# An MLP's up-projection by Strassen's scheme, and a down-projection of its own

## The chip, the cores and the metric

The kernel runs on one core of a Trainium2 chip. A core has five engines that run side by side, each with its own queue of instructions: TensorE (PE, matmuls, with the loads of its weights shown as PEld), VectorE (DVE), ScalarE (ACT), GpSimd (POOL) and SyncE (SP), which here issues the DMAs. They wait for one another by semaphores. The metric is the device time of one execution in microseconds (us); lower is better.

## The reference, cut to what matters

One encoder layer over 2048 tokens of 1024 features, in float32. The mixer and the cross-attention come first and are not touched. What is changed is the MLP behind them, with 4096 hidden features:

```python
def sq_relu_mlp(x, mlp_norm, w_up, w_down):
    h = rms_norm(x, mlp_norm) @ w_up          # 2048 x 1024 @ 1024 x 4096
    return jnp.square(jax.nn.relu(h)) @ w_down  # 2048 x 4096 @ 4096 x 1024

x = x + sq_relu_mlp(x, mlp_norm[l], w_up[l], w_down[l])
return rms_norm(x, final_norm)
```

## The kernel before, in words

Activations lie with features on the 128 partitions and tokens along the row. Float32 accuracy is made from reduced-precision operands: `split` (L108) turns a tensor into a high part (a cast on ACT, L110) and a low part, the remainder (a subtraction on DVE, L111), and `mm3` (L136) makes of each product three matmuls: high by high, high by low, low by high (L138 to L140). A matmul has 128 contracted rows and up to 512 columns.

The MLP (L952 on) takes the 2048 tokens in two halves (`hf`) of 1024, each of two blocks of 512. A half goes through 16 groups of two hidden feature tiles (128 features each). In a group, the up-projection makes one PSUM tile per hidden tile and block: 8 k-tiles by 3 matmuls. ACT takes the ReLU out of PSUM (L994), DVE multiplies it with the positive part (L996), and the result is split. Then the down-projection: for each block and each of the 8 output tiles `d`, 2 x 3 matmuls into PSUM, which DVE adds to a running sum in SBUF (L1029). These sums `acc` begin as the residual, which the cross-attention has stored in DRAM as `x2d`. Both weight matrices are loaded (512 KB a tile, L124) and split once per half, so twice in all.

The token operands are the normalised blocks. The 1/rms of a block is made by squares on ACT (`fold`, L177), their sums on GpSimd (L181), a small matmul (L154), a power on GpSimd (L146) and a broadcast by matmul (L162); the final norm does the same with squares of L1035 and sums of L1039. For the MLP's input, `prep_step` (L195) multiplies the block by it (L199) and splits it. For the first half this is done before the cross-attention's end: the loads, the products and the splits of block 0, and the first weights, stand ahead of `xa_last` (L717), the last piece of the cross-attention, which adds into the residual (L727) and stores it (L728). For the second half it is spread over the last groups of the first (L1004 to L1013, L1030 to L1032).

The order of the instructions is made by the framework's scheduler, which keeps one static queue for each engine; buffers come from pools of tiles with a fixed number of buffers, and a tile that is to be written waits for the last reader of the one that had the place before. PSUM has eight banks, four of the tag `ps` and four of `pg`. SP issues all loads and stores in one order, and an issue that waits holds up those behind it.

The lines that the prediction's steps touch:

```python
L110  mark["act"] = nc.scalar.copy(hi, src)
L111  nc.vector.tensor_tensor(out=lo, in0=src, in1=hi.bitcast(F32), op=ALU.subtract)
L994  nc.scalar.activation(r, ps, AF.Relu)
L996  nc.vector.scalar_tensor_tensor(out=u, in0=ps, scalar=0.0, in1=r, op0=ALU.max, op1=ALU.mult)
L1029 nc.vector.tensor_tensor(out=acc[d][:, cs], in0=ps, in1=acc[d][:, cs], op=ALU.add)
```

Of the kernel before, what the change touches and what calls it, by code (L numbers as in the profile page):

```python
# [30 lines left out]
def block_kernel(ctx, tc, x, mem, wm, wv, wlg, wlog, wout, wxk, wxv, wxqT, wxo, wup, wdn,  # L31
# [3 lines left out]
    big = ctx.enter_context(tc.tile_pool(name="big", bufs=1))  # L35
# [38 lines left out]
    # ---- constants  # L74
# [14 lines left out]
    nc.vector.tensor_copy(oneb, one)  # L89
    nhalf = cpool.tile([P, 16], F32, name="nhalf")  # L90
    nc.vector.memset(nhalf, -0.5)

    # ---- scratch in DRAM
# [8 lines left out]
    x2d = dram.tile([D, S], F32, name="x2d")  # L102

# [45 lines left out]
    def rstd_col(sq, PT):  # L149
        """sums of squares over the features, left on each partition -> 1 / rms, tokens on partitions"""  # L150
# [6 lines left out]
    def to_rows(rc, PT):  # L157
        """one value per token, tokens on partitions -> the same on all partitions"""
# [13 lines left out]
    def fold(tiles, SQ, eng):  # L172
        """squares of the tiles [P, 2, n], summed up"""
# [20 lines left out]
    def prep_step(res, gain, r, kp, xt):  # L194
        """two feature tiles of a block of 512 tokens, normalised: hi and lo [P, 2 kt, 512]"""  # L195
# [8 lines left out]
    # =========================== in-projection ===========================  # L204
# [4 lines left out]
    def mtiles(tiles, blks, ws=None):  # L209
        """tiles: (index, evac); the whole group for one block, then for the other one"""  # L210
# [44 lines left out]
    def vg(hf, blks, nxt, meanwhile=None):  # L255
        """columns of v and of silu(g), 256 at a time"""
# [8 lines left out]
    def lr_g(hf, blks):  # L265
        """low-rank gate inputs (rows f at 0..15, ones at 16, b at 32..47, b one token late) and g's first columns"""
# [32 lines left out]
    def conv(hf, blks, cs, ws=None, meanwhile=None):  # L299
        # y = B * dwconv3(C * u), channels on partitions  # L300
# [4 lines left out]
        def group(c, ws):  # L305
# [16 lines left out]
            def taps():  # L322
                # T[i] is the convolution at token (t0 + i) in the first half, (t0 - 2 + i) in the second
# [42 lines left out]
    # =========================== gated linear attention ===========================  # L366
    def gla_decay(h, res):
        """decayed k and q, rows 0..63 for the forward scan and 64..127 for the backward one; in stages"""
# [5 lines left out]
        # log_sigmoid(z) = min(z, 0) - ln(1 + exp(-|z|))  # L374
# [14 lines left out]
        def sums(hf):  # L389
# [5 lines left out]
            # sums run from token 0 and from token 64 of a chunk; both become distances to token 63  # L395
# [28 lines left out]
        # decay from one chunk's middle to the next one's  # L424
# [539 lines left out]
    for hf in range(2):  # L964
# [11 lines left out]
        for g in range(NG_):  # L976
            fs = range(G * g, G * g + G)
            if g > 0:
                ws = [load_w(wup[f]) for f in fs]
# [128 lines left out]
```

## Time and profile before

| what | value |
|---|---|
| three runs, us | 2854.97, 2857.62, 2862.69 (median 2857.62) |
| span of the profiled execution, first to last instruction, us | 2856.6 |
| mean granted TensorE clock | 0.983 of full speed |
| TensorE busy, us | 2756.2 (96%) |
| from the MLP's first matmul to the end, us | about 1435 |
| matmuls from 1422 us to the end | 6291 recorded |
| DVE, ACT and POOL busy from 1422 us to the end, us | 720, 317, 69 |
| DMA from 1422 us to the end | 20% busy, 62 GB/s |

The profiled execution is known by its span; the record of it holds no other time, and the span lies between the lowest and the highest of the three runs. A busy share alone does not say what sets the time: TensorE is nearly always busy, so what counts is how many matmuls there are, at what pitch they follow one another, and where TensorE stops.

### The profile page before, as it was taken

The numbers are of one execution on the slowest core, as the hardware profiler recorded it, in microseconds if no ns is written. First come the engines' busy times: TensorE is split into PE (matmuls) and PEld (weight loads), VectorE is DVE, ScalarE is ACT, GpSimd is POOL, SyncE is SP. The second block draws the span as 40 slices with busy tenths as digits, with TensorE's granted clock in tenths as the row PEclk, the third lists the DMA queues.
The fourth block names the chain that finished last, engine by engine and source line by source line (L and its number), as shares of the span: only waits on it lengthen the run. The fifth ranks groups of instructions, "written<-read, shape, count | busy, mean of one in ns | idle before, by whom it ended". The sixth has DMA issues, their size and how long they took to land.

```text
span 2856.6 us, 34634 instructions
## 1 busy us (share of the span) xinstructions
PE 2756.2 (96%) x14232; PEld 2352.7 (82%) x14232; DVE 1413.6 (49%) x2177; ACT 811.6 (28%) x1222; POOL 183.9 (6%) x149
## 2 busy tenths in 40 slices
PE   7999989988989999999999999999999999999997
PEld 6898878877777889999988888888878888888886
DVE  6413372556766544343554544444575454444444
ACT  5411162423445433221321121122232122112122
POOL 1000010302200000000200000002030000000003
PEclk9999999998999999999999999999999999999999
DMA  7412363234445441101621111122153111112111
GB/s 239 157 62 67 109 221 115 88 92 116 129 125 186 144 157 45 60 31 59 214 74 45 45 59 45 45 60 88 60 162 104 45 45 59 45 45 59 45 37 60
DMA packets 140383, 259.92 MB, mean 91 GB/s; under 512 B 12672, under 2 KB 69120, under 8 KB 140224
## 3 DMA queue, kind: packets, MB, share of 16 engines
q1 hardware_dynamic: 140224, 257.70, 28.8%
q8 instruction: 111, 1.82, 0.3%
q14 instruction: 48, 0.39, 0.0%
HBM read 203.13 MB, written 54.53 MB: 90 GB/s over the span
## 4 chain that ended last, share of the span: by engine, by line
PE 64%; issue 2%; DVE 2%; ACT 1%; POOL 1%; DMA 1%; SPq 0%; POOLq 0%; DVEq 0%; ACTq 0%
PE ps L138 11%; PE ps L139 11%; PE ps L140 11%; PE pg L140 10%; PE pg L138 10%; PE pg L139 10%; POOL gt L1039 0%; PE pg L698 0%; DMA raw<-zy 0%; DVE a L111 0%; POOL sm L146 0%; DVE raw L199 0%; PE ps L162 0%; DMA raw<-in_wout 0%; ACT L590 0%
## 5 line engine op out<-in xcount | busy, mean ns | idle before, releaser
L138 PE MATMUL ps<-a,a 128*128 128x512 f32 (+1 forms) x1864 | 706.3, 379 | 7.4 <-DVE t L242 6.7
L139 PE MATMUL ps<-a,a 128*128 128x512 f32 (+1 forms) x1864 | 705.6, 379 | 0.0
L140 PE MATMUL ps<-a,a 128*128 128x512 f32 (+1 forms) x1864 | 704.1, 378 | 0.0
L110 ACT CAST a<-raw 128x1024 fp32r<-128x1024 f32 (+1 forms) x216 | 219.5, 1033 | 702.1 <-PE pg L140 508.1
L138 PEld LDWEIGHTS ps<-a,a 128*128 128x128 f32 x1864 | 354.6, 190 | 74.1 <-DVE t L242 6.2
L111 DVE TENSOR_TENSOR a<-raw,a 128x1024 fp32r<-128x1024 f32 (+1 forms) x216 | 263.5, 1225 | 291.2 <-PE ps L139 205.6
L139 PEld LDWEIGHTS ps<-a,a 128*128 128x128 f32 x1864 | 355.0, 190 | 63.1 <-issue 0.2
L140 PEld LDWEIGHTS ps<-a,a 128*128 128x128 f32 x1864 | 354.7, 190 | 63.4 <-issue 0.4
L138 PE MATMUL pg<-gt,a 128*128 128x512 f32 (+1 forms) x880 | 302.8, 344 | 0.0
L140 PE MATMUL pg<-gt,a 128*128 128x512 f32 (+1 forms) x880 | 302.8, 344 | 0.0
L139 PE MATMUL pg<-gt,a 128*128 128x512 f32 (+1 forms) x880 | 302.7, 344 | 0.0
L1029 DVE TENSOR_TENSOR g<-pg,g 128x512 f32<-128x512 f32 (+1 forms) x260 | 177.3, 683 | 148.0 <-PE pg L140 147.9
L1029 DVE TENSOR_TENSOR st<-pg,st 128x512 f32<-128x512 f32 (+1 forms) x260 | 176.7, 681 | 118.5 <-PE pg L140 118.4
L138 PE MATMUL pg<-g,a 128*128 128x512 f32 (+1 forms) x552 | 213.8, 387 | 3.1 <-DVE st L1029 2.8
L139 PE MATMUL pg<-g,a 128*128 128x512 f32 (+1 forms) x552 | 213.4, 387 | 0.0
L140 PE MATMUL pg<-g,a 128*128 128x512 f32 (+1 forms) x552 | 213.3, 386 | 0.0
L994 ACT ACTIVATE t<-ps 128x512 f32<-128x512 f32 x128 | 76.6, 599 | 424.6 <-PE ps L140 424.6
L996 DVE SCALAR_TENSOR_TENSOR t<-ps,t 128x512 f32<-128x512 f32 x128 | 88.1, 688 | 204.2 <-ACT t L994 204.2
L138 PEld LDWEIGHTS pg<-gt,a 128*128 128x128 f32 x880 | 166.9, 190 | 20.2 <-DVE gt L111 0.3
L139 PEld LDWEIGHTS pg<-gt,a 128*128 128x128 f32 x880 | 167.0, 190 | 19.9
L140 PEld LDWEIGHTS pg<-gt,a 128*128 128x128 f32 x880 | 167.1, 190 | 19.6
L138 PEld LDWEIGHTS pg<-g,a 128*128 128x128 f32 x552 | 103.8, 188 | 24.6 <-DVE st L1029 3.1
(284 smaller groups left out, 3755.3 us busy)
## 6 DMA issues: line engine op xcount, KB each, us to landing
raw<-in_wup SPq DMA_DIRECT2D x64, 512.0 KB, 3.6
raw<-in_wdn SPq DMA_DIRECT2D x64, 512.0 KB, 3.9
raw<-in_wm SPq DMA_DIRECT2D x32, 512.0 KB, 4.1
raw<-x2d SPq DMA_DIRECT2D x48, 256.0 KB, 3.8
a<-in_x SPq DMA_DIRECT2D x32, 256.0 KB, 6.4
gt<-zv SPq DMA_DIRECT2D x32, 256.0 KB, 3.4
raw<-zy SPq DMA_DIRECT2D x32, 256.0 KB, 4.0
raw<-in_wv SPq DMA_DIRECT2D x12, 512.0 KB, 4.6
```

Of the source, the lines that this page charges most:

```text
L110: mark["act"] = nc.scalar.copy(hi, src)
L111: nc.vector.tensor_tensor(out=lo, in0=src, in1=hi.bitcast(F32), op=ALU.subtract)
L138: nc.tensor.matmul(ps, lh, rh, start=first, stop=False)
L139: nc.tensor.matmul(ps, lh, rl, start=False, stop=False)
L140: mark["pe"] = nc.tensor.matmul(ps, ll, rh, start=False, stop=last)
L994: nc.scalar.activation(r, ps, AF.Relu)
L996: nc.vector.scalar_tensor_tensor(out=u, in0=ps, scalar=0.0, in1=r, op0=ALU.max, op1=ALU.mult)
L1029: nc.vector.tensor_tensor(out=acc[d][:, cs], in0=ps, in1=acc[d][:, cs], op=ALU.add)
```

## The change

The MLP is made anew, in two stages with pools of their own. The pool `big` of the earlier parts is closed ahead of it; a tile of the new pool waits for the last users of the bytes that it takes.

**The up stage** still goes through two halves of 1024 tokens. In a half the product is cut in two in each dimension: tokens into two blocks of 512, the contracted features into two halves of 512, and hidden tiles into pairs, `f` and `f + 16`. The eight block products become seven by Strassen's scheme (in Winograd's form), each of 4 k-tiles by 3 matmuls. That asks for sums and differences of the operands. `token_side` makes the seven token operands of a half once: it loads four quarters (512 features by 512 tokens, 1 MB), normalises them on DVE, makes four sums or differences of 128x2048 on GpSimd, and splits all seven. `weight_side` makes the seven weight operands of a pair `f`: two loads of 512 KB, four DVE additions of 128x512, and splits of 1024 columns three times and 512 once. Its tiles `h8` have four buffers, three of which a pair takes. The four results are put together from PSUM by one ACT copy and five DVE additions, taken through the squared ReLU on ACT or DVE, and stored in a DRAM scratch `zu`, four times 256 KB a pair. The second half's 1/rms is made at pairs 12 and 15 of the first half; its operands are made when the second half asks for them.

**The down stage** goes once over all 2048 tokens: 16 groups of two hidden tiles; each hidden tile loads 1 MB of `zu` and 512 KB of `w_down`, both split again; 8 output tiles by 4 blocks by 2 x 3 matmuls add to eight running sums of 128x2048, which are loaded from `x2d` at the stage's start. The final norm comes in the last group, for blocks of 512, 512, 512, 256 and 256 tokens.

The other parts of the diff: `rows`, a tile for the two 1/rms of a half; comments taken out; and a smaller scratch for dynamic DMA descriptors (`dynamic_dma_scratch_size=1024`).

```diff
             xa_probs(s, 1)
-            for kp in range(4):
-                prep_step(blks[0], g_mlp, rs[0], kp, load_T(x2d, 0, kp, XR(kp)))
-            ws = [load_w(wup[f]) for f in range(2)]
             xa_last(s)
-            for kp in range(4):
-                prep_step(blks[1], g_mlp, rs[1], kp, load_T(x2d, 1, kp, XR(kp)))
             continue
...
+    phase.close()
+    up = phase.enter_context(tc.tile_pool(name="up", bufs=1, reuse_waits="tile"))
...
+    def quarter(b, k):
+        t = W8(4, TB)
+        nc.sync.dma_start(t, x2d[k * TB:(k + 1) * TB, b * TB:(b + 1) * TB].rearrange("(j p) t -> p j t", p=P))
+        return t
...
+    def token_side(hf):
+        def norm(b, k):
+            t = quarter(2 * hf + b, k)
+            for j in range(4):
+                kt = 4 * k + j
+                nc.vector.scalar_tensor_tensor(out=t[:, j], in0=t[:, j], scalar=g_mlp[:, kt:kt + 1],
+                                               in1=rows[:, b], op0=ALU.mult, op1=ALU.mult)
+            return t
+        a11 = norm(0, 0)
+        yield 1, operand(a11)
+        a21, a22 = norm(1, 0), norm(1, 1)
+        s = W8(4, TB)
+        add(s, a21, a22, eng=nc.gpsimd)
+        yield 5, operand(s)
+        add(s, s, a11, ALU.subtract, eng=nc.gpsimd)
+        yield 6, operand(s)
+        a12 = norm(0, 1)
+        yield 2, operand(a12)
+        add(a21, a11, a21, ALU.subtract, eng=nc.gpsimd)
+        yield 7, operand(a21)
+        yield 4, operand(a22)
+        add(a12, a12, s, ALU.subtract, eng=nc.gpsimd)
+        yield 3, operand(a12)
+
+    def weight_side(f):
+        raw = W8(2, 1024)
+        for i in range(2):
+            nc.sync.dma_start(raw[:, i], wup[f + 16 * i])
+        w11, w21, w12, w22 = raw[:, 0, :TB], raw[:, 0, TB:], raw[:, 1, :TB], raw[:, 1, TB:]
+        t = W8(4, TB)
+        ha, hb, hc, hd = H8(), H8(), H8(), H4()
+        split(raw[:, 0], ha[:, 0], ha[:, 1])
+        add(t[:, 0], w12, w11, ALU.subtract)
+        add(t[:, 1], w22, t[:, 0], ALU.subtract)
+        split(t[:, 0:2].rearrange("p a b -> p (a b)"), hb[:, 0], hb[:, 1])
+        add(t[:, 2], w22, w12, ALU.subtract)
+        add(t[:, 3], t[:, 1], w21, ALU.subtract)
+        split(t[:, 2:4].rearrange("p a b -> p (a b)"), hc[:, 0], hc[:, 1])
+        split(w22, hd[:, 0], hd[:, 1])
...
+            product(px, W[1], x(1), True)
+            c1 = U2()
+            nc.scalar.copy(c1, px)
+            product(pz, W[5], x(5), True)
+            product(py, W[6], x(6), True)
+            u2 = U2()
+            add(u2, py, c1)
+            product(px, W[2], x(2), False)
+            c11 = U2()
+            sq_relu(c11, px, f, b0)
+            product(py, W[7], x(7), False)
+            add(c1, py, c1)
+            c22 = U2()
+            add(c22, pz, c1)
+            sq_relu(c22, c22, f + 16, b1)
+            product(pw, W[4], x(4), True)
+            add(c1, c1, pw, ALU.subtract)
+            sq_relu_v(c1, f, b1)
+            product(pz, W[3], x(3), False)
+            add(u2, pz, u2)
+            sq_relu_v(u2, f + 16, b0)
...
+    nxt = dn_load(0)
+    acc = []
+    for d in range(KT):
+        acc.append(dn_tile((S,), "acc", KT))
+        nc.sync.dma_start(acc[d], x2d[d * P:(d + 1) * P, :])
```

Three places where the queues now differ. In the rows, a line's number is that of its own kernel (L114 of the changed one is L111 of the one before), and the arrow goes from what is read to what is written.

**SP's queue at the cross-attention's end.** `raw` and `cv` are row buffers of the old pool, `w8` the 1 MB buffers of the new one. Before:

```order
L124 DMA raw_11740<-in_wup 128x1024
L169 DMA cv_11971<-x2d_92 128x512 x2
L124 DMA raw_11746<-in_wup 128x1024
L169 DMA cv_11989<-x2d_92 128x512 x2
L169 DMA raw_11962<-x2d_92 128x512 x2
L169 DMA raw_11980<-x2d_92 128x512 x2
L124 DMA raw_12142<-in_wdn 128x1024
L728 DMA x2d_92<-raw_11054 128x4x256
L728 DMA x2d_92<-cv_11058 128x4x256
```

Changed:

```order
L731 DMA x2d_93<-raw_11056 128x4x256
L731 DMA x2d_93<-cv_11060 128x4x256
L1037 DMA w8_11918<-in_wup 128x1024 x2
L1037 DMA w8_11938<-in_wup 128x1024 x2
L980 DMA w8_11962<-x2d_93 128x4x512
L980 DMA w8_11986<-x2d_93 128x4x512
L980 DMA w8_11992<-x2d_93 128x4x512
L980 DMA w8_12035<-x2d_93 128x4x512
```

The MLP's first weights and token blocks were issued ahead of the last two stores of the residual, and now stand behind them.

**DVE's queue at the same place.** `a4` are the operands of before, `c8` the token operands of now (one row is the low part of one operand), `u2` the results. Before, with the eight additions of L727 (the last of the cross-attention) between:

```order
L199 SCALAR_TENSOR_TENSOR raw_11980<-raw_11980,vec_67,a4_11476 128x512 x2
L111 TENSOR_TENSOR a4_11966<-raw_11962,a4_11965 128x1024
L727 TENSOR_TENSOR raw_11054<-pg_11752,raw_11054 128x256
...
L727 TENSOR_TENSOR cv_11058<-ps_11759,cv_11058 128x256
L111 TENSOR_TENSOR a4_11975<-cv_11971,a4_11974 128x1024
L111 TENSOR_TENSOR a4_11984<-raw_11980,a4_11983 128x1024
L111 TENSOR_TENSOR a4_11993<-cv_11989,a4_11992 128x1024
```

Changed, after those eight additions (L730) and the weights of the first two pairs:

```order
L1014 SCALAR_TENSOR_TENSOR w8_11962<-w8_11962,vec_67,rows_73 128x512 x4
L1014 SCALAR_TENSOR_TENSOR w8_11986<-w8_11986,vec_67,rows_73 128x512 x3
L114 TENSOR_TENSOR c8_11969<-w8_11962,c8_11968 128x2048
L1014 SCALAR_TENSOR_TENSOR w8_11986<-w8_11986,vec_67,rows_73 128x512
L1014 SCALAR_TENSOR_TENSOR w8_11992<-w8_11992,vec_67,rows_73 128x512 x4
L114 TENSOR_TENSOR c8_12001<-w8_11998,c8_12000 128x2048
L1014 SCALAR_TENSOR_TENSOR w8_12035<-w8_12035,vec_67,rows_73 128x512 x4
L114 TENSOR_TENSOR c8_12018<-w8_11998,c8_12017 128x2048
L114 TENSOR_TENSOR c8_12042<-w8_12035,c8_12041 128x2048
L114 TENSOR_TENSOR c8_12063<-w8_11986,c8_12062 128x2048
L975 TENSOR_TENSOR u2_12033<-pg_11959,u2_11984 128x512
```

What was done for the first half on both sides of the cross-attention's last additions now stands wholly behind them, and the low parts of the operands 5, 6 and 7 (`c8_12001`, `c8_12018`, `c8_12063`) stand behind sums that GpSimd makes.

**DVE's queue in the middle of a half.** Before, one group: the squared ReLUs, the splits and the running sums.

```order
L996 SCALAR_TENSOR_TENSOR t2_12386<-ps_12359,t2_12384 128x512
L111 TENSOR_TENSOR g4_12388<-t2_12386,g4_12388 128x512
L111 TENSOR_TENSOR a4_12573<-raw_12570,a4_12572 128x1024
L996 SCALAR_TENSOR_TENSOR t2_12418<-ps_12391,t2_12416 128x512
L1029 TENSOR_TENSOR st_11998<-pg_12436,st_11998 128x512
L111 TENSOR_TENSOR gt_12421<-t2_12418,gt_12420 128x512
```

Changed, one pair (`u2_12415` is the sum `c1`, `u2_12472` is `c22`, `u2_12441` is `u2`; `h8_12384` and `h8_12385` are the operands `hb` and `hc` of the next pair, `w8_12766` the weight sums of a later one, `h8_12511` the `ha` of the pair after the next):

```order
L975 TENSOR_TENSOR u2_12441<-pg_12400,u2_12415 128x512
L114 TENSOR_TENSOR h8_12384<-w8_12382,h8_12384 128x1024
L114 TENSOR_TENSOR h8_12385<-w8_12382,h8_12385 128x1024
L975 TENSOR_TENSOR w8_12766<-w8_12763 128x512
L975 TENSOR_TENSOR u2_12415<-pg_12400,u2_12415 128x512
L975 TENSOR_TENSOR w8_12766<-w8_12763,w8_12766 128x512
L975 TENSOR_TENSOR u2_12472<-ps_12401,u2_12415 128x512
L975 TENSOR_TENSOR w8_12766<-w8_12763 128x512
L975 TENSOR_TENSOR w8_12766<-w8_12766,w8_12763 128x512
L975 TENSOR_TENSOR u2_12415<-u2_12415,pg_12402 128x512
L114 TENSOR_TENSOR h8_12511<-w8_12507,h8_12511 128x1024
L1067 SCALAR_TENSOR_TENSOR u2_12415<-u2_12415 128x512
```

DVE's work of a pair is now a row of small sums and splits in a fixed order, in which the sum `c22`, read out of the PSUM tile that the last product of the pair adds to, stands behind the low parts of `hb` and `hc` and two weight sums.

More of the change, by code (lines that the diff above doesn't have):

```diff
@@ L89, in block_kernel @@
     nc.vector.tensor_copy(oneb, one)
+    rows = cpool.tile([P, 2, TB], F32, name="rows")
     nhalf = cpool.tile([P, 16], F32, name="nhalf")
@@ new lines, in C8, with H8, H4, U2 @@
+    def C8():
+        return up.tile([P, 4, TB], F32R, tag="c8", name="c8", bufs=14)
+    def H8():
+        return up.tile([P, 2, 1024], F32R, tag="h8", name="h8", bufs=4)
+    def H4():
+        return up.tile([P, 2, TB], F32R, tag="h4", name="h4", bufs=2)
+    def U2():
+        return up.tile([P, TB], F32, tag="u2", name="u2", bufs=6)
+    def US(n):
+        return up.tile([P, 16], F32, tag="us", name="us", bufs=4)[:, :n]
+    def add(out, a, b, op=ALU.add, eng=nc.vector):
+        eng.tensor_tensor(out=out, in0=a, in1=b, op=op)
@@ new lines, in block_rstd, with operand @@
+    def block_rstd(sq, PT, out):
+        ps = PT()
+        for i in range(4):
+            nc.tensor.matmul(ps[:, i:i + 1], sq[:, i * P:(i + 1) * P], onec, start=True, stop=True)
+        nc.scalar.copy(out, to_rows(rstd_of(ps[:, :4], 4, D, lambda n: US(n), nc.vector), PT))
+    def operand(src):
+        hi, lo = C8(), C8()
+        split(src, hi, lo)
+        return hi, lo
+    def token_side(hf):
[21 more added lines that the diff above has]
+        yield 3, operand(a12)
@@ new lines, in product, with sq_relu @@
+    def product(ps, W, X, first):
+        for kt in range(4):
+            ks = slice(kt * P, (kt + 1) * P)
+            for w, x in ((0, 0), (0, 1), (1, 0)):
+                nc.tensor.matmul(ps, W[w][:, ks], X[x][:, kt], start=first and kt + w + x == 0,
+                                 stop=kt == 3 and w == 1, skip_group_check=not first)
+    def sq_relu(t, src, f, b):
+        nc.scalar.activation(t, src, AF.Relu)
+        nc.scalar.activation(t, t, AF.Square)
+        nc.sync.dma_start(zu[f * P:(f + 1) * P, b * TB:(b + 1) * TB], t)
@@ new lines, in sq_relu_v, with x @@
+    def sq_relu_v(t, f, b):
+        nc.vector.scalar_tensor_tensor(out=t, in0=t, scalar=0.0, in1=t, op0=ALU.max, op1=ALU.mult)
+        nc.sync.dma_start(zu[f * P:(f + 1) * P, b * TB:(b + 1) * TB], t)
+    early = None
+    for hf in range(2):
+        b0, b1 = 2 * hf, 2 * hf + 1
+        X = {}
+        side = token_side(hf)
+        W = weight_side(0)
+        for f in range(16):
+            def x(i):
+                if i not in X:
+                    k, X[k] = next(side)
+                    assert k == i
+                return X[i]
+            nxt = weight_side(f + 1) if f + 1 < 16 else None
+            px, py, pz, pw = PS(), PG(), PS(), PG()
+            product(px, W[1], x(1), True)
[19 more added lines that the diff above has]
+            sq_relu_v(u2, f + 16, b0)
+            W = nxt
+            if hf == 0 and f == 12:
+                early = [squares(2), squares(3)]
+            if hf == 0 and f == 15:
+                for i, sq in enumerate(early):
+                    block_rstd(sq, PG, rows[:, i])
@@ L956, in final_norm @@
+    nxt = dn_load(0)
[3 more added lines that the diff above has]
+        nc.sync.dma_start(acc[d], x2d[d * P:(d + 1) * P, :])
+    def final_norm(cs, n, PT, sq):
+        m = n // P
+        ps = PT()
+        for i in range(m):
+            nc.tensor.matmul(ps[:, i:i + 1], sq[:, i * P:(i + 1) * P], onec, start=True, stop=True)
+        r = to_rows(rstd_of(ps[:, :m], m, D, lambda k: dn_tile((16,), "ds", 4)[:, :k], nc.vector), PT)
         for d in range(KT):
```

165 lines of the change are left out of this document (74 added, 91 removed).

## The prediction

> **What bounds the kernel now.** I read the page's first and fourth parts, then windows of 200 us, then the waits of TensorE in the MLP, then the timeline at the two places where the MLP's stages meet.
>
> ```profile
> span 2856.6 us, 34634 instructions
> PE 2756.2 (96%) x14232; PEld 2352.7 (82%) x14232; DVE 1413.6 (49%) x2177; ACT 811.6 (28%) x1222; POOL 183.9 (6%) x149
> 1600.00:1800.00 200.00, 200.00 (x884) 165.58 (x883) 94.00 (x127) 41.71 (x58) 0.00 (x0) 1.00 0.17 52
> 1800.00:2000.00 200.00, 200.00 (x884) 165.62 (x883) 94.55 (x126) 44.98 (x59) 19.65 (x8) 1.00 0.21 64
> ```
>
> In the windows the columns are the stretch, its length, then busy time and instructions of PE, PEld, DVE, ACT and POOL, the granted clock, the DMA share and GB/s. TensorE never stops there and starts 884 matmuls in 200 us: one per 0.2262 us. DVE is busy for 94 of 200, DMA for a fifth. So a matmul taken out is worth 0.2262 us, if nothing else begins to set the pace.
>
> TensorE stops in the MLP where the halves meet:
>
> ```profile
> 2127.00:2140.00 13.00, 8.30 (x31) 6.96 (x30) 7.50 (x12) 1.57 (x2) 6.91 (x5) 0.74 0.63 203
> 2132.89 1.98 PE L162 MATMUL pg<-cst,sm 128*128 128x128 f32 x8 [4.70 <-POOL sm L146]
> 2136.80 0.63 PE L140 MATMUL ps<-a,a 128*128 128x512 f32 x1
> 2137.23 0.63 PE L138 MATMUL ps<-a,a 128*128 128x512 f32 x1
> ```
>
> It stands for 4.70 us, and the matmuls behind it follow at 0.43 us for a while, at a granted clock of 0.74 over the 13 us. At the MLP's start it hardly stops:
>
> ```profile
> 1422.90 0.47 PE L138 MATMUL ps<-a,a 128*128 128x512 f32 x1 [0.66 <-DVE raw L727]
> 1424.78 0.37 SPq L728 DMA_DIRECT2D x2d<-cv  x1
> ```
>
> **What goes.** The up-projection had 16 x 3 matmuls a hidden tile and half (two blocks, 8 k-tiles), that is 96 a pair of tiles; seven products of 12 make 84. Over 32 pairs that is 384 fewer of 128x512, the same form as before: 384 x 0.2262 = **-86.9**. The down-projection keeps its 3072. The stop between the halves: in those 13 us stand 13 full matmuls (2.9 us), and the small ones of two rows at about 2; some 8 us were lost, at least the 4.70 of the wait: **-7**.
>
> **What comes: the price list.** All new vector work has nearby rows.
>
> ```profile
> L111 DVE TENSOR_TENSOR a<-raw,a 128x1024 fp32r<-128x1024 f32 x122 | 153.2, 1257 | 139.9 <-PE ps L139 115.8 <-ACT a L110 21.8 <-POOL a L181 2.3
> L110 ACT CAST a<-raw 128x1024 fp32r<-128x1024 f32 x121 | 124.4, 1049 | 507.3 <-PE pg L140 470.5 <-PE pg L139 18.3 <-PE ps L139 10.1
> L111 DVE TENSOR_TENSOR g<-t,g 128x512 fp32r<-128x512 f32 x58 | 40.2, 693 | 37.8 <-ACT g L110 37.8
> L110 ACT CAST g<-t 128x512 fp32r<-128x512 f32 x58 | 36.0, 621 | 31.4 <-DVE t L996 30.3
> 1424.66 1.22 DVE L111 TENSOR_TENSOR a<-cv,a 128x1024 fp32r<-128x1024 f32 x1
> 1425.79 1.23 DVE L111 TENSOR_TENSOR a<-raw,a 128x1024 fp32r<-128x1024 f32 x1
> 2132.81 1.26 POOL L1039 TENSOR_TENSOR gt<-gt 128x512 f32<-128x512 f32 x1
> L181 POOL TENSOR_TENSOR a<-a,a 128x1024 f32<-128x1024 f32 x6 | 15.3, 2544 | 582.4 <-ACT a L177 582.2
> 2134.91 2.72 DVE L957 SCALAR_TENSOR_TENSOR st<-st,vec,pg 128x512 f32<-128x512 f32 x4 [5.50 <-PE pg L162]
> raw<-in_wup SPq DMA_DIRECT2D x64, 512.0 KB, 3.6
> ```
>
> In the groups the last figures before the bar are busy us and mean ns. Back to back a DVE operation costs less than its duration (1.13 between the two starts of 1424.66 and 1425.79). Doubling columns from 512 to 1024 adds 0.43 us on ACT, 0.56 on DVE and 1.28 on POOL; so 128x2048, which no row shows, is estimated at 1.9 us on ACT, 2.2 to 2.4 on DVE and 4.8 on POOL. Four normalising products take 2.7.
>
> **Start of the up stage.** T is the end of the cross-attention's last matmul. Before, operands of the first block and the first weights were ready by then; now SP issues the weights only behind the store of the residual, which waits for DVE's additions: T+1. Landing at 3.6 and more: T+5.6. DVE then works in its queue's order. The weights of two pairs come first (four low parts of 1024, two of 512, eight sums): 10.6 us with the first cast's 1, to 17.2. The token loads land by 15.8 and are covered by that. Then the chain: products a11 and most of a21 with the low part of operand 1, 24.3; a21 and a22, 27.6; GpSimd's sum s, 32.4; cast of operand 5, 34.4, its low part; s minus a11, again 4.8 on GpSimd; cast and low part of 6, low part of 2, low part of 7; GpSimd's last difference; cast and low part of 3; the sum `c22`; then pair 0's last product. With GpSimd's and DVE's operations at their undisturbed or mildly lengthened prices this ends at T+66. One row says more on the disturbance:
>
> ```profile
> 2115.43 3.52 POOL L1039 TENSOR_TENSOR gt<-gt 128x512 f32<-128x512 f32 x2 [0.90 <-ACT gt L1035]
> 2115.60 2.21 DVE L111 TENSOR_TENSOR a<-raw,a 128x1024 fp32r<-128x1024 f32 x1
> ```
>
> DVE's 1.23 became 2.21 beside two GpSimd sums. If it waited out the first (2115.43 + 1.26 = 2116.69) and then ran 1.13, it ends at 2117.82; it ends at 2117.81, and the second sum, started then, at 2119.07 against 2118.95. So I take it that these operations wait for one another in full. The low part of 5 then waits for the difference of operand 7 (37.2, done 39.4), the low parts behind the last difference wait likewise, and the end moves to T+68.8. TensorE had 9 products to do in that time, 9 x 12 x 0.2262 = 24.4 us; 0.7 was lost before too. Loss: 68.8 - 24.4 - 0.7 = **+44**. Ends: 32, if four of the links overlap that I put in a row, and 54, if each of eleven handovers costs about 1 us more than I gave it.
>
> The Trainium skill, page "SBUF — State Buffer", section "Who interferes with whom", says that DVE's second pair of ports is GpSimd's own, and that a DVE instruction with two SBUF inputs contends with GpSimd, the one that began first keeping the pair. The two rows above agree with that at 1.26 us; no row shows it at 4.8. By the rule the sum is the one below; by a mere slowing it would be 5 us less.
>
> **Start of the second half.** Its operands are asked for when its first product is: the same chain, without the first wait for weights. The 1/rms rows come first, through DVE, GpSimd's power, broadcasts and a copy:
>
> ```profile
> 2125.50 0.95 PE L154 MATMUL pg<-vec,gt 128*128 128x1 f32 x8
> 2131.82 1.02 POOL L146 TENSOR_TENSOR sm<-sm,nhalf 128x4 f32<-128x4 f32 x1
> ```
>
> They are there 4.5 and 9.0 us after the last product, the first operand is whole at 14, and the chain from there is as long: T+57.9. Less 24.4 of products, and about 4.2 for the small matmuls of two blocks (0.95 for eight of L154, up to 1.98 for eight broadcasts), which the kernel before has as well: **+29** (20 to 38).
>
> **Start of the down stage.** Its first weights and `zu` tiles stand on SP behind the last store of the up stage, which waits for the pair's last sum. 1 MB at the 394 GB/s of the busiest quoted stretch takes 2.7 us:
>
> ```profile
> 1395.00:1400.00 5.00, 4.48 (x40) 4.25 (x39) 3.07 (x8) 2.67 (x7) 1.01 (x1) 1.00 1.04 394
> ```
>
> Weights at 5.8, `zu` 8.3, cast 9.3, low part 10.5; then TensorE begins at the slow clock that followed the 4.70 us wait above, some 1.7 us more: **+12** (8 to 20). The eight 1 MB running sums land from 16 to 36 us; PSUM's eight banks and TensorE's 1.36 us a tile cover the first of them.
>
> **Steady state.** A pair is 84 matmuls, 19.0 us. DVE has three low parts of 1024, one of 512, nine sums of 0.6 to 0.7 and two multiplications: 11.5 us, hidden. What counts is order: the pair's last product adds to the PSUM tile that `c22` reads. With time from the pair's first matmul: `hc`'s buffer is freed at 11.14, cast 12.18, low part 13.34, a weight sum, `c1` 14.54, a weight sum, `c22` done at 15.83. The last product is due at 16.32. Spare: 0.5 us. So nothing, and **+4** (0 to 8) for the first pairs of each half, where DVE is behind. DMA is 2 MB per 19 us, 105 GB/s, well under 394; the down stage asks for 3 MB a group of 43 us.
>
> Sum: -86.9 - 7 + 44 + 29 + 12 + 4 = -4.9. From the span of 2856.6 that is 2851.7; the median of the runs lies 1.0 above the span, so **2853 us**, nearly no change. Its own range, from the ends of the terms, is 2836 to 2869. A measurement of this kernel cannot tell changes under 0.3%, 8.6 us: no change is 2849 to 2866.
>
> **The rivals.**
>
> *The stage starts are cheaper.* Links overlap: lower ends halfway for all three starts, -6, -5 and -2, and DVE and GpSimd merely slow one another, -5: 2835. For it: I summed handovers in a row. Against: every queue's order is fixed, and the two rows fit waiting.
>
> *The last product waits in every pair.* The spare is 0.5 us over six handovers, between a PSUM read and a product:
>
> ```profile
> 1645.82 0.39 PE L140 MATMUL ps<-a,a 128*128 128x512 f32 x1
> 1646.31 0.60 ACT L994 ACTIVATE t<-ps 128x512 f32<-128x512 f32 x1 [4.18 <-PE ps L140]
> 1646.94 0.69 DVE L996 SCALAR_TENSOR_TENSOR t<-ps,t 128x512 f32<-128x512 f32 x1 [3.93 <-ACT t L994]
> ```
>
> From the last matmul's start to its reader is 0.49, ACT to DVE 0.03; two operations of DVE ahead of `c22` more than I put (1.2 us) eat the spare and leave 0.75 a pair; over the 28 pairs behind the first ones +21: 2874, slower. It decides from about 0.3 us a pair on. Against: two such sums would have to change places.
>
> *The running sums come late.* If the loads of 8 MB go behind weights and `zu` of the next group, block 0's additions stop the eight banks until 36 us: +13, 2866.
>
> That the change does not do what it says is excluded: the queue of TensorE holds the 2688 matmuls of the up stage, and their form is that of before.
>
> **Chances.** Forecast 0.46, cheaper starts 0.20, waiting last product 0.20, late sums 0.08, something else 0.06. Faster by over 0.3% (under 2849): 0.18 of the forecast's share, 0.18 of the cheaper starts', 0.02: 0.38. Within 0.3%: 0.23, 0.02, 0.05 of the others: 0.30. Slower: 0.05, 0.20, 0.07: 0.32. Range over both rivals: 2829 to 2880.
>
> **What would show it.** 884 matmuls per 200 us in the middle of both stages show the first term right. TensorE's waits should be in three clusters: about 45 us behind the start of the up stage, the largest for low parts of operands 5, 6 and 3 and for GpSimd; about 29 at the second half; about 12 ahead of the first down-projection. Low parts of 2048 columns beside GpSimd should take the rest of GpSimd's operation longer. A wait of the pair's last product for `c22` in most pairs shows the second rival. Wrong it would be if a cluster is under half of that, or if matmuls of the up stage follow at another pitch.

## The result, and the profile after

The changed kernel takes 2863.5 us (median of 18 runs), the kernel before 2855.7 us in the same comparison: a ratio of 1.0023, interval 1.0015 to 1.0030. It is slower by 0.23%, within the 0.3% that the prediction called no change, inside the range, and on the other side of the forecast, which was nearly no change with a small gain (-4.9 us on the profiled execution).

The page of the changed kernel, its first part, and windows (stretch, length, then busy time and instructions of PE, PEld, DVE, ACT and POOL, granted clock, DMA share, GB/s). The first two lie in the middle of the up stage's second half and of the down stage:

```profile
span 2861.8 us, 34708 instructions
PE 2688.0 (94%) x13848; PEld 2286.7 (80%) x13848; DVE 1584.1 (55%) x2367; ACT 844.8 (30%) x1216; POOL 220.0 (8%) x157
1862.00:2062.00 200.00, 200.00 (x884) 165.59 (x883) 113.69 (x155) 69.45 (x95) 0.00 (x0) 1.00 0.31 104
2500.00:2700.00 200.00, 200.00 (x884) 165.59 (x883) 129.15 (x174) 29.01 (x30) 0.00 (x0) 1.00 0.20 70
1418.50:1500.50 82.00, 46.49 (x169) 35.02 (x170) 68.26 (x68) 30.70 (x30) 20.57 (x4) 0.77 0.45 157
1671.80:1695.00 23.20, 20.64 (x86) 16.58 (x85) 12.98 (x12) 11.72 (x12) 14.68 (x7) 0.94 0.54 182
1771.50:1846.70 75.20, 54.62 (x202) 42.65 (x201) 59.60 (x58) 27.16 (x27) 23.47 (x6) 0.77 0.34 111
```

The pitch held: 884 matmuls in 200 us in both stages. There are 384 fewer (13848 for 14232), and with them 87 us are gone. The last three windows are places where TensorE stopped: the first two pairs of the first half took 82.0 us for 168 matmuls that need 38.1, pair 11 took 23.2 us for 19.0, and from the end of the first half to the end of the second half's first two pairs passed 75.2 us, again for 38.1.

TensorE's waits in the whole MLP (waiter, releaser: total us, times, longest):

```profile
PE ps L1058 <- ACT c L113: 35.3, 6, 22.1
PE pg L141 <- ACT uh L113: 10.2, 1, 10.2
PE pg L165 <- POOL ds L149: 9.2, 2, 5.3
PE ps L1058 <- DVE c L114: 8.6, 4, 2.4
PE ps L165 <- POOL ds L149: 7.2, 3, 3.6
...
PE ps L1058 <- DVE u L975: 2.6, 1, 2.6
```

The first and the fourth are the up stage's starts (as are the rows left out above the last), the second is the start of the down stage. The third and the fifth, 16.4 us together, are the final norm waiting for GpSimd; they lie at the end, and the prediction has no term for them. The last row is the only wait of a product for the sum `c22`, once, at pair 11.

I kept a ledger of lost time: the length of a stretch less its matmuls at the pitch, 0.2266 us each. The MLP itself, from the cross-attention's last matmul to the end, went from 1434.4 us (2856.6 - 1422.2) to 1443.3 us (2861.8 - 1418.5), so by +8.9. (The part ahead of it has the same 7944 matmuls in both and took 3.7 us less in this execution. I don't count that as the change: in all the profiled executions of this document that part ends between 1415.8 and 1422.8 us, in the three kernels with the old MLP between 1417.5 and 1422.2.)

| us | before | changed | difference | predicted |
|---|---|---|---|---|
| matmuls taken out | | | -87.0 | -86.9 |
| start of the up stage | 0.7 | 43.9 | +43.2 | +44 |
| pair 11, squares of the second half | 0 | 4.3 | +4.3 | 0 (+4 for the first pairs, none seen) |
| 1/rms and start of the second half | 5.8 | 37.1 | +31.3 | +29 |
| start of the down stage | 0 | 13.3 | +13.3 | +12 |
| stop between the halves | 11.8 | 0 | -11.8 | -7 |
| final norm in the last group | 14.3 | 30.6 | +16.3 | 0 |
| after the last matmul | 7.9 | 7.4 | -0.5 | 0 |
| sum | | | +9.1 | -4.9 |

Five rows are as the prediction has them, within 2.5 us: the matmuls, the three starts and the end. Pair 11 comes to what I had put for the first pairs, but that is luck, since place and cause are others. The stop between the halves is 4.8 us larger than I put, because the ledger counts the small matmuls of the norm in it, and the last group is what the prediction left out.

A row is good to some 3 us. Five of the profiled kernels share the code of the up stage, the changed one and four in which only the last group is altered; their ledgers give 43.5 to 46.6 us for the first start and 32.6 to 37.0 for the second. Nor is a loss the same as a wait: at the two starts of the changed kernel TensorE waits for 56.1 of the 81 us. Small matmuls are 6.6 more, and the rest, about 18, is lost by matmuls that follow a stop at more than 0.2266 us each, with a granted clock of 0.77 in both windows.

The stop between the halves and the end of the kernel before, and the end of the changed one, as windows:

```profile
2122.60:2146.00 23.40, 18.70 (x85) 15.80 (x84) 13.47 (x20) 6.09 (x9) 11.92 (x9) 0.85 0.55 180
2822.80:2857.00 34.20, 18.27 (x129) 17.11 (x127) 19.22 (x44) 7.19 (x18) 15.41 (x20) 0.80 0.35 123
2801.00:2862.00 61.00, 35.72 (x210) 32.28 (x208) 34.20 (x70) 11.31 (x26) 26.33 (x29) 0.81 0.39 138
```

GpSimd (the last pair before the clock) is busy for 11.9 and 15.4 us in the first two, and for 26.3 in the third.

### The profile page after: what moved, and what is told of

The parts are those of the page before. It is cut to its first block, busy times and chain, and to the rows that moved or that the text cites. A ratio compares the mean times of both kernels' runs of the same rounds, so it can differ in the third digit from the quotient of the medians.

```text
span 2861.8 us, 34708 instructions
## 1 busy us (share of the span) xinstructions
PE 2688.0 (94%) x13848; PEld 2286.7 (80%) x13848; DVE 1584.1 (55%) x2367; ACT 844.8 (30%) x1216; POOL 220.0 (8%) x157
## 5 line engine op out<-in xcount | busy, mean ns | idle before, releaser
L1058 PE MATMUL ps<-c,h 128*128 128x512 f32 x1536 | 375.7, 400 | 49.0 <-ACT c L113 35.3
L1058 PEld LDWEIGHTS ps<-c,h 128*128 128x128 f32 x1536 | 296.4, 194 | 117.6 <-ACT c L113 37.5
L141 PE MATMUL ps<-a,a 128*128 128x512 f32 (+1 forms) x840 | 305.3, 363 | 6.7 <-DVE t L245 6.7
L142 PE MATMUL ps<-a,a 128*128 128x512 f32 (+1 forms) x840 | 304.8, 363 | 0.0
L143 PE MATMUL ps<-a,a 128*128 128x512 f32 (+1 forms) x840 | 303.7, 362 | 0.0
L1058 PE MATMUL pg<-c,h 128*128 128x512 f32 x1152 | 275.2, 392 | 6.2 <-DVE c L114 3.4
L1058 PEld LDWEIGHTS pg<-c,h 128*128 128x128 f32 x1152 | 217.4, 189 | 53.4 <-DVE c L114 4.5
L975 DVE TENSOR_TENSOR acc<-ps,acc 128x512 f32<-128x512 f32 (+1 forms) x260 | 176.5, 680 | 121.6 <-PE ps L143 121.1
L975 DVE TENSOR_TENSOR acc<-pg,acc 128x512 f32<-128x512 f32 (+1 forms) x260 | 176.6, 680 | 119.5 <-PE pg L143 117.6
L141 PE MATMUL pg<-uh,wh 128*128 128x512 f32 (+1 forms) x520 | 201.9, 389 | 11.0 <-ACT uh L113 10.2
L141 PE MATMUL ps<-uh,wh 128*128 128x512 f32 (+1 forms) x520 | 202.0, 389 | 1.0 <-DVE acc L1151 1.0
L142 PE MATMUL pg<-uh,wh 128*128 128x512 f32 (+1 forms) x520 | 201.8, 388 | 0.0
L143 PE MATMUL pg<-uh,wh 128*128 128x512 f32 (+1 forms) x520 | 201.7, 388 | 0.0
L142 PE MATMUL ps<-uh,wh 128*128 128x512 f32 (+1 forms) x520 | 201.6, 388 | 0.0
L143 PE MATMUL ps<-uh,wh 128*128 128x512 f32 (+1 forms) x520 | 201.5, 388 | 0.0
L114 DVE TENSOR_TENSOR h<-w,h 128x1024 fp32r<-128x1024 f32 (+1 forms) x128 | 152.4, 1193 | 62.8 <-ACT h L113 62.8
L141 PEld LDWEIGHTS ps<-a,a 128*128 128x128 f32 x840 | 160.7, 191 | 33.0 <-DVE t L245 6.3
L143 PEld LDWEIGHTS ps<-a,a 128*128 128x128 f32 x840 | 160.8, 191 | 23.2 <-issue 0.4
L142 PEld LDWEIGHTS ps<-a,a 128*128 128x128 f32 x840 | 160.9, 192 | 22.9 <-issue 0.2
L114 DVE TENSOR_TENSOR a<-raw,a 128x1024 fp32r<-128x1024 f32 (+1 forms) x76 | 88.3, 1173 | 133.2 <-PE ps L142 73.3
```

The costliest lines, as they stand in the source:

```text
L141: nc.tensor.matmul(ps, lh, rh, start=first, stop=False)
L142: nc.tensor.matmul(ps, lh, rl, start=False, stop=False)
L143: mark["pe"] = nc.tensor.matmul(ps, ll, rh, start=False, stop=last)
L975: eng.tensor_tensor(out=out, in0=a, in1=b, op=op)
L1058: nc.tensor.matmul(ps, W[w][:, ks], X[x][:, kt], start=first and kt + w + x == 0, stop=kt == 3 and w == 1, skip_group_check=not first)
```

## The experiments

**Theory at the outset.** The stop between the halves was for the most part the final norm of the first half; the change did not remove it but moved it to the last group, which now has the norms of four blocks of 512 tokens where it had two. There GpSimd, which sums the squares and makes the power, is too slow for it. Rivals: VectorE's products or the stores set the end; or the starts of the stages cost more than they seem to, for reasons other than the chain of sums.

The end of the changed kernel, on the timeline:

```profile
2812.49 8.09 POOL L975 TENSOR_TENSOR q<-q 128x512 f32<-128x512 f32 x6 [7.45 <-ACT q L1175]
2815.63 0.16 DVE L147 TENSOR_SCALAR ds<-pg 128x4 f32<-128x4 f32 x1
2820.53 1.02 POOL L149 TENSOR_TENSOR ds<-ds,nhalf 128x4 f32<-128x4 f32 x1
2821.61 1.67 PE L165 MATMUL pg<-cst,ds 128*128 128x128 f32 x8 [3.87 <-POOL ds L149]
2823.38 5.36 DVE L1151 SCALAR_TENSOR_TENSOR acc<-acc,vec,pg 128x512 f32<-128x512 f32 x8 [5.78 <-PE pg L165]
```

The mean of one block is ready at 2815.8, but its power begins at 2820.5, behind six sums of the next block; TensorE waits 3.87 us for it in its own order.

**The power ahead of the sums.** The norm of a block goes into the next block's loop.

```diff
                         add(sq, sq, q, eng=nc.gpsimd)
-            for fn in late:
-                fn()
+                if d == 3:
+                    for fn in late:
+                        fn()
+                    late = []
```

> The changed kernel with one edit: in the last group of the down stage, the final norm of a block is put into the next block's loop after its fourth output tile, not after its eighth. Nothing is left out. Theory: the 8.9 us by which the MLP got longer come from the final norm, which in the changed kernel costs 16 us more at the end (the two more blocks now have it there); what is late in it is GpSimd's power, queued behind six sums of squares of the next block (1.26 us each, ready at 2815.6 us, begun at 2820.5). With two sums ahead of it, TensorE's waits of 3.9, 3.0 and 5.3 us for it shrink: 10 to 14 us less than the changed kernel, 2850 to 2853 us, 0.998 to 0.9995 of the kernel before. Rival: the end is set by VectorE's products and the stores of the result, whose total does not change: within 3 us of the changed kernel, about 2862.

Measured: 2867.4 us, 1.0031 (1.0018 to 1.0043), no gain. The waits for the power fall from 16.4 to 2.6 us, and others, 12.1 us for the sums themselves, stand in their place:

```profile
2818.85 5.36 DVE L1151 SCALAR_TENSOR_TENSOR acc<-acc,vec,pg 128x512 f32<-128x512 f32 x8 [2.71 <-PE pg L165]
2825.68 6.82 POOL L975 TENSOR_TENSOR q<-q 128x512 f32<-128x512 f32 x6 [7.83 <-ACT q L1175]
2831.07 1.05 PE L1148 MATMUL ps<-vec,q 128*128 128x1 f32 x8 [3.36 <-POOL q L975]
2855.24 1.01 PE L1148 MATMUL ps<-vec,q 128*128 128x1 f32 x4 [4.28 <-POOL q L975]
```

VectorE's eight products stand ahead of the additions, so GpSimd has nothing to sum for 7.83 us and then is late with the sums themselves. My first form of the theory, the place of the power, falls; GpSimd's total remained.

**The same edit in the kernel before.**

> The kernel before with the same edit of the final norm as in e1_tail: after the next block's fourth output tile. Nothing is left out. In the kernel before the final norm costs 14 us in its last group. Theory: the same queue of GpSimd is at work, so some of it goes too, 3 to 6 us, 2851 us, 0.9985. Rival: with only three blocks behind one another the norm is not late there, no change, 1.000.

Measured: 2859.7 us, 1.0010 (1.0001 to 1.0020). No gain here either, rather a loss of 3 us. That agrees with the rival as far as it goes, and with the miss of the run above.

**No sums at all.** The line that adds the squares on GpSimd is taken out, in the changed kernel and in the kernel before.

```diff
-                    else:
-                        add(sq, sq, q, eng=nc.gpsimd)
```

> The changed kernel without GpSimd's sums of squares in the final norm: only the squares of the first output tile go into the 1/rms, so the output is scaled wrongly; nothing else is left out. Putting the norm earlier (e1_tail) only moved the wait from the power to the sums, so the second form of the theory is: GpSimd's seven sums and a power of a block (7 x 1.26 + 1.0 = 9.8 us, and 5.8 for a block of 256) take nearly all of the 10.9 us (5.4) that TensorE needs for it, and VectorE's eight products in a row (5.4 us) hold up the additions that feed them, so that nothing is made good. Without the sums the final norm costs 14 us or less instead of 30.6: 2845 to 2850 us, 0.997. Rival (the products of VectorE alone are in the way): 5 us less at most, 2858 or more.

> The kernel before without GpSimd's sums of squares in its final norm, as e5_nosums was of the changed one: only the first output tile's squares count, so the output is scaled wrongly. A control: the kernel before pays for its final norm at two places, 14.3 us at the end and most of the 11.8 us between the halves. If both are the same waiting for GpSimd, it gains there 8 to 12 us, 2847 us, 0.9965, and the stop between the halves was the norm of the first half, which the change moved and did not remove. If the stop has another cause (the next half's operands), it stays, and 3 to 5 us go: 2853, 0.9985.

Measured: the changed kernel 2848.7 us, 0.9973 (0.9963 to 0.9982); the kernel before 2847.5 us, 0.9971 (0.9960 to 0.9983). Without the sums the two kernels are equal to within their intervals. The ledger says where: in the changed kernel the last group's loss falls from 30.6 to 15.1 us (the time after the last matmul grows by 3), in the kernel before that of the last group only from 14.3 to 13.6, but that between the halves from 11.8 to 4.5. The wait there, 4.70 us in the prediction's row, is now

```profile
2124.31 1.16 PE L162 MATMUL pg<-cst,sm 128*128 128x128 f32 x8 [0.70 <-POOL sm L146]
```

So the stop between the halves was the waiting for GpSimd's sums of the first half's final norm, and this waiting is what the change put, doubled, into the last group.

**Fewer sums, more small matmuls.** GpSimd sums the squares of five of the eight tiles, TensorE adds the rest.

```diff
-                    if sq is None:
-                        sq = q
-                    else:
-                        add(sq, sq, q, eng=nc.gpsimd)
+                    if 0 < d <= 4:
+                        add(parts[0], parts[0], q, eng=nc.gpsimd)
+                    else:
+                        parts.append(q)
...
+            for k, q in enumerate(parts):
+                nc.tensor.matmul(ps[:, i:i + 1], q[:, i * P:(i + 1) * P], onec, start=k == 0, stop=k == len(parts) - 1)
```

> The changed kernel with a final norm that asks less of GpSimd: it sums the squares of output tiles 0 to 4 (four sums for seven), TensorE adds up the rest by more small matmuls in PSUM (16 for 4 a block of 512, 0.12 us each, 1.4 us more), the power is put after the third tile of the next block, and rows and products after its fifth. Nothing is left out. If GpSimd's rate sets the tail: about 16 us less, 6 us more for TensorE, 2850 to 2856 us, 0.9985. If the products are in the way: as the changed kernel or slower by the 6 us, 2865 to 2870.

Measured: 2865.3 us, 1.0032 (1.0019 to 1.0046). A miss, with its price on the timeline:

```profile
2794.96 3.85 PE L1149 MATMUL ps<-vec,q 128*128 128x1 f32 x32
```

The 16 small matmuls are 32 instructions and take 3.85 us where 8 took 0.95: 2.9 us more a block of 512, 11.6 in all, and not the 6 I had put. The ledger's loss at the end is 33.0 us with these, so by its time alone the run fits the rival. TensorE's waits for GpSimd at the end tell more:

```profile
PE ps L165 <- POOL ds L149: 1.7, 2, 1.1
PE ps L1149 <- POOL q L975: 0.9, 1, 0.9
PE pg L165 <- POOL ds L149: 0.3, 1, 0.3
```

They are 2.9 us in all, for 16.4 in the changed kernel and 14.7 in the run that only put the norm earlier. With fewer sums the waiting for GpSimd went, as the theory has it, and the small matmuls took its place.

**Twice the time a block.** The last two groups of the down stage are made as one: four hidden tiles a block, so that a block lasts 21.8 us while its norm asks the same of GpSimd and VectorE.

```diff
-        last = g == NG_ - 1
+        last = g == NG_ - 2
+        if last:
+            us, ws = us + nxt[0], ws + nxt[1]
...
-                for j in range(G):
+                for j in range(len(us)):
```

> The changed kernel with the last two groups of the down stage made as one: a block of tokens is taken through all four hidden tiles (12 matmuls an output tile, one addition) before the next block, so that a block lasts 21.8 us and not 10.9 while its final norm stays as it is; the norm is put after the third output tile of the next block. Nothing is left out. If the final norm is late because GpSimd's 9.8 us and VectorE's 10 us a block find no slack beside 10.9 us of matmuls, all but the last block's norm goes under the matmuls: 16 to 20 us less than the changed kernel, 2845 us, 0.996. If the waits come from the order of the queues alone, they come back once a block as before: 2860.

Measured: 2845.2 us, 0.9961 (0.9948 to 0.9975), 18 us less than the changed kernel. The end of it, as a window from 2770 us on and by TensorE's waits in it:

```profile
2770.00:2851.00 81.00, 69.74 (x421) 61.46 (x419) 38.69 (x75) 15.57 (x31) 32.63 (x33) 0.94 0.29 104
...
PE ps L1148 <- POOL q L975: 2.0, 1, 2.0
PE ps L165 <- POOL ds L149: 1.6, 2, 1.1
PE pg L165 <- POOL ds L149: 0.2, 1, 0.2
```

The waits for GpSimd are 3.8 us in all, for 16.4 before, and the loss by the ledger is 12.7 us for 30.6. GpSimd's 40 instructions of the norm take as long as before (41.7 us from 2743 us on here, 41.4 from 2780 us on in the changed kernel), but beside 87 us of matmuls and not 43.5. By itself the run doesn't tell GpSimd from VectorE, since both have twice the time and VectorE half the additions. The runs without sums do: the sums on GpSimd are 15.5 of the 30.6 us. So the mechanism is this: a block of the last group has 10.9 us of matmuls; beside it GpSimd needs about 10 us for seven sums and a power, and VectorE 5.4 us for the products and 5.5 for the additions. Each waits for the other, so nothing that is late is made good.

**The starts: the sums on VectorE.** The four token sums of a half are made on VectorE.

```diff
-        add(s, a21, a22, eng=nc.gpsimd)
+        add(s, a21, a22)
```

(and the same for the other three)

> The changed kernel with one edit: the four token sums of a half are made on VectorE, not on GpSimd. Nothing is left out. Theory (VectorE and GpSimd wait for one another in full, and GpSimd's 4.55 us a sum stands in the chain): three sums in the chain at 2.2 instead of 4.55 us, and VectorE's waits of 2.5, 4.4 and 3.8 us beside GpSimd go, against one sum more on VectorE: about 12 us less at the start of each half, 24 in all, 2840 us, 0.994. Rival (the waits are only those for the casts and the order of the queue): three times 2.3 less one sum of 2.2 more, about 5 us a half, 2853 us, 0.999.

Measured: 2842.0 us, 0.9952 (0.9937 to 0.9966): 20 us less than the changed kernel by the ratios (0.0071 x 2856), 9.6 at the first start and 10.7 at the second by the ledger. The theory said 24, its rival 10. The rows of the changed kernel, VectorE beside GpSimd:

```profile
1457.76 4.99 POOL L975 TENSOR_TENSOR w<-w,w 128x2048 f32<-128x2048 f32 x1 [2.23 <-DVE c L114]
1457.60 7.02 DVE L1014 SCALAR_TENSOR_TENSOR w<-w,vec,rows 128x512 f32<-128x512 f32 x4
1469.34 6.54 POOL L975 TENSOR_TENSOR w<-w,w 128x2048 f32<-128x2048 f32 x1 [6.59 <-DVE c L114]
1471.93 5.04 DVE L114 TENSOR_TENSOR h<-w,h 128x1024 fp32r<-128x1024 f32 x1
```

and with the sums on VectorE, the same place:

```profile
1446.38 4.62 DVE L975 TENSOR_TENSOR w<-w,w 128x2048 f32<-128x2048 f32 x2
1453.11 0.75 DVE L1014 SCALAR_TENSOR_TENSOR w<-w,vec,rows 128x512 f32<-128x512 f32 x1
1455.98 2.07 DVE L1014 SCALAR_TENSOR_TENSOR w<-w,vec,rows 128x512 f32<-128x512 f32 x3
1465.31 1.22 DVE L114 TENSOR_TENSOR h<-w,h 128x1024 fp32r<-128x1024 f32 x1
```

Four products that take 2.8 us took 7.02 beside a sum (4.99 us here; two of them back to back take 9.11), and a low part of 1.22 us took 5.04: the wait is for the whole of GpSimd's operation, at 128x2048 too. The sum that takes GpSimd about 4.6 us takes VectorE 2.3. The Trainium skill, page "SBUF — State Buffer", section "Who interferes with whom", says that a VectorE instruction with two SBUF inputs contends with GpSimd's reads, and that who comes first keeps the shared ports for the whole instruction; these rows agree with it, at nearly four times the length that the kernel before showed.

**The starts: without Strassen's scheme.** The two stages are kept, with eight plain products a pair.

```diff
-            product(pz, W[5], x(5), True)
-            product(py, W[6], x(6), True)
-            u2 = U2()
-            add(u2, py, c1)
...
+            product(px, W[2], x(2), False)
+            sq_relu(U2(), px, f, b0)
+            product(py, W[3], x(1), True)
+            product(py, W[4], x(2), False)
+            sq_relu(U2(), py, f + 16, b0)
```

> The changed kernel with its two stages, but without Strassen's scheme: eight block products a pair (96 matmuls for 84), the four normalised quarters and the weights split as they are, no sums on either side, all four results through ScalarE. Nothing is left out. It tells what the sums cost, apart from the stages and the way through DRAM. Theory: 87 us more of matmuls; at the start of each half the chain is shorter by the sums and three splits, about 25 us in the first and 19 in the second less than the 43.6 and 37.0 of the changed kernel; the squares' stop of 4.4 us stays or falls: 2900 to 2910 us, 1.016 to 1.019. Rival (the starts are long because of the loads and the new pools, not of the sums): the starts keep most of their length, 2935 us or more, 1.028.

Measured: 2904.4 us (two runs), 1.0170 (1.0149 to 1.0190), as the theory said. By the ledger the starts cost 22.4 and 15.0 us (43.9 and 37.1 with the sums), pair 11 nothing, the start of the down stage 13.3 and the last group 31.0, as before. So of the 87 us that the scheme takes from TensorE, its operands (the sums, and the splits that come with them) give 48 back: 21.5 at the first start, 22.1 at the second and 4.3 at pair 11. What is left of the starts isn't of the scheme; no run shows how much of it is the new pools, the loads behind the last stores, or the splits.

**The starts: earlier loads.** The first loads of the up and of the down stage are issued on ScalarE's queue.

```diff
-        nc.sync.dma_start(t, x2d[
+        (nc.scalar if b < 2 else nc.sync).dma_start(t, x2d[
...
-        W = weight_side(0)
+        W = weight_side(0, nc.sync if hf else nc.scalar)
...
-            nc.sync.dma_start(w, wdn[f])
+            (nc.sync if g else nc.scalar).dma_start(w, wdn[f])
```

> The changed kernel with the first loads of the up stage (weights of pair 0 and the four quarters of the first half) and of the down stage (the first two tiles of weights and of the hidden activations) issued from ScalarE's queue, where they do not stand behind the last stores. The buffers that they take are free earlier. Nothing is left out. Theory: VectorE begins the weights at the cross-attention's end instead of 5.6 us later, 5 less at the first start; the down stage begins some 8 us earlier, of which the running sums' loads, still behind the stores, take back 2 or 3: 2852 us, 0.9985. Rival (the starts are set by VectorE's chain and by the loads of the running sums): under 4 us less, 2860.

Measured: 2863.0 us, 1.0023 (1.0012 to 1.0034), no gain: the rival. TensorE's waits at the two starts:

```profile
1436.94 0.79 PE L1058 MATMUL ps<-c,h 128*128 128x512 f32 x1 [16.92 <-ACT c L113]
1440.63 4.71 PE L1058 MATMUL ps<-c,h 128*128 128x512 f32 x11 [2.90 <-DVE c L114]
2117.54 0.79 PE L141 MATMUL pg<-uh,wh 128*128 128x512 f32 x1 [5.89 <-ACT uh L113]
2131.66 0.79 PE L141 MATMUL pg<-uh,wh 128*128 128x512 f32 x1 [5.15 <-ACT uh L113]
```

At the first start the first wait fell by 5.1 us, as the theory has it, but the ledger there only by 1.8 (42.1 us for 43.9), which is within its spread. The down stage began 4.3 us earlier and then stopped 5.15 us for its second hidden tile. The chain behind that stop:

```profile
2112.39 7.75 DMA wr<-in_wdn
...
2120.15 0.37 ACT wh L113
...
2120.56 9.93 DMA ur<-zu
```

The load of that tile now stands in ScalarE's queue behind the cast of the second weights. It was issued at 2120.56, 7 us behind the first of the running sums' loads (2113.54, on SyncE's queue); in the changed kernel it was issued at 2116.74, ahead of them. So TensorE waits for the tile and not for the running sums, but their loads, 8 MB, had overtaken it.

**All of these at once.**

> The token sums on VectorE (2842 us alone), the squares of the second half's 1/rms summed on VectorE too (the stop of 4.4 us at pair 11), the final norm of e7_tail2 and the early loads of e8_early, all in one. Nothing is left out. If the gains add: 2842 - 4 - 8 - 10 = 2820 us, 0.9875. If the starts' gains overlap, since one VectorE chain sets both, and the tail does not move: 2835, 0.993.

Measured: 2840.4 us, 0.9940 (0.9925 to 0.9955), near the second reading: the first start lost 29.7 us, the second 23.9, pair 11 0.7, but the start of the down stage 16.6 and the last group 31.4, since these two edits had gained nothing alone. The 0.7 shows one small thing: with the squares summed on VectorE, pair 11's stop of 4.3 us is gone.

**The best of them.** The sums and squares on VectorE, the early loads of the up stage alone, and the merged last groups.

> The same with the token sums and the squares of the second half on VectorE and the up stage's first loads on ScalarE's queue (the down stage's stay on SyncE's, where they began no later for good in e8_early: the running sums' loads took back what they won). Nothing is left out. From e9_all's 2840: its final norm of 31 us falls to about 12, its start of the down stage from 16.6 to 13: 2817 us, 0.986. If the merged groups do not help: 2837.

Measured: 2817.6 us, 0.9866 (0.9852 to 0.9881), as forecast. It beats the kernel before by 38 us, the changed one by 45. TensorE's largest waits in it:

```profile
PE ps L1058 <- ACT c L113: 26.9, 6, 16.8
PE pg L141 <- ACT uh L113: 10.1, 1, 10.1
PE ps L1058 <- DVE c L114: 5.7, 3, 2.9
```

The starts are what remains: 31.3 us at the first, 26.4 at the second, 13.3 at the down stage.

## Why the prediction was wrong

**What bounds the kernel, and the matmuls taken out.** Right: -87.0 for -86.9, the pitch unchanged.

**Start of the up stage.** Right in size (+43.2 for +44) and in its chain: the low part of operand 1 ended at T+24.3, GpSimd's sum at 32.4, the cast of operand 5 at 34.4 and its low part at 39.2, where I had 24.3, 32.4, 34.4 and 39.4. I had the wrong releasers in part: TensorE waits for the casts of operands 1 (22.1 us) and 5 (5.6) and for low parts of 5, 4 and 1 (2.3, 1.7 and 1.5), and not for the low parts of 6 and 3. The reading that VectorE and GpSimd wait for one another in full was taken from two rows of 1.26 us and held at 4.6; the run with the sums on VectorE gives the 20 us of it, where I had 24.

**Start of the second half.** +31.3 for +29, within the ledger's spread. (By the figures given there the end is T+58.5, 14 and the 44.5 us from T+24.3 to T+68.8, and not T+57.9.)

**Start of the down stage.** +13.3 for +12. That the running sums' loads are covered held too: no wait for them appears among TensorE's (VectorE waits 2.2 us for them).

**Steady state.** Right: but for pair 11 no product waits for `c22`; the rival of the last product is refuted. The +4 that I put for the first pairs of a half was not there; a stop of 4.3 us at pair 11 was, which I had not seen: the squares of the second half's 1/rms stand in ScalarE's queue, wait there for their load, and the casts of the next weights are behind them. (The program asks for them at pair 12; the scheduler put them earlier.)

```profile
1674.76 2.40 POOL L975 TENSOR_TENSOR w<-w 128x1024 f32<-128x1024 f32 x1 [10.12 <-ACT w L988]
1675.17 2.54 DVE L114 TENSOR_TENSOR h<-w,h 128x512 fp32r<-128x512 f32 x1 [1.74 <-ACT h L113]
1677.73 2.63 SPq L980 DMA_DIRECT2D w<-x2d  x2
1682.84 1.92 ACT L988 ACTIVATE w<-w 128x2048 f32<-128x2048 f32 x1 [7.22 <-DMA w<-x2d]
1684.66 1.98 ACT L113 CAST h<-w 128x1024 fp32r<-128x1024 f32 x2
```

The load is late in its turn, since it waits for a low part that took 2.54 us beside a GpSimd sum. With these sums on VectorE (the last run above) that low part takes 0.68 us, and one of the casts stands ahead of the square; no run tells which of the two ends the stop.

**The stop between the halves, the step that failed.** I counted its 4.70 us and the slow matmuls behind it as removed, -7, and wrote nothing on where the work behind it goes. (The ledger's 11.8 us for the stop hold the norm's small matmuls too, some 5 us, which I had put aside.) The row itself said what it was: the broadcast of the final norm (L162) waiting for GpSimd's power. The final norm of the first half isn't removed by the change but moved to the last group, and I costed the move at nothing without naming the work that would hide it. Nothing does: beside a block's 10.9 us of matmuls GpSimd is busy for about 10 us with the norm, and VectorE for 10.9 with its products and the additions. The last group lost 30.6 us in place of 14.3. Together the two rows of the ledger are +4.5 where I had -7, which is 11.5 of the 14.0 us between the forecast and the ledger; the rest is 2.3 at the second half, 1.3 at the down stage, and small terms that cancel. GpSimd's sums make the difference: in the two kernels without them the same rows are 4.5 and 13.6 us before and 15.1 after, together -3.0 (about 0 with the 3 us more after the last matmul) and not +4.5.

**The rivals.** "The stage starts are cheaper" did not come: they were dearer by 3 us. "The running sums come late": not seen. The slower side came by a mechanism that none of the rivals named; it falls under "something else", to which I had given 0.06.

## What to carry to other kernels

A stall that vanishes with a change of order has to be followed to the work that caused it: if the work is still done, write down where, and whether the engine that was late has more time there. A tail stage is best given as much matmul time per block as its slowest helper needs, for example by putting two accumulation groups into one; this was worth 18 us where moving the late instruction within its queue was worth nothing. And fewer matmuls by sums of operands pay only if the sums are off the path: here 48 of 87 us came back, and 20 of these were saved by taking the sums from the slower of two engines that block one another.

## What the runs showed of the hardware that was not expected

A VectorE operation beside a GpSimd sum of 4.6 us took 5.04 us instead of 1.22: the wait grows with the other engine's whole operation. A matmul of one column in float32 is two instructions here, 0.12 us each. Not settled: why the norm earlier in the next block costs the kernel before 3 us; its wait went from the power to the sums as in the changed kernel, but no run tells that apart from the order of VectorE's queue.
